# A decoder step on one Trainium2 core: the sample rows' new SSM states formed in the second feed-forward block, and their readout in the mixer from the old states

## The chip, the core and the metric

The kernel runs on one core of a Trainium2 chip. A core has a matmul engine (TensorE, PE in the profile; its weight loads are the row PEld), VectorE (DVE), ScalarE (ACT), GpSimd (POOL) and SyncE (SP), which here issues transfers. Each engine works through its own queue of instructions in order, and engines wait for one another on semaphores. The metric is the device time of one execution in microseconds. Three runs of the kernel before took 1035.49 to 1036.48 us, with a median of 1035.54 us.

## What is computed

One step of a decoder trunk: a half-step SwiGLU feed-forward block, a mixer of two parallel parts (causal pooling, and a Mamba-2 state space part with 16 heads), a second feed-forward block, and a last norm. It runs on 512 prompt rows and on 8 sample rows that each carry a state from earlier steps. Prompt and sample rows are columns of the same tiles: 512 + 8 = 520 columns, in two halves of 260. All inputs and outputs are float32.

```python
def _trunk(x, ...):
    h = h + 0.5 * _swiglu(_rms_norm(h, ffn1_norm[l]), ...)
    m, p, c, s = _hybrid_mixer(_rms_norm(h, mix_norm[l]), ...)
    h = h + m
    h = h + 0.5 * _swiglu(_rms_norm(h, ffn2_norm[l]), ...)
...
def step(h, inp):
    s, a = inp
    return a[..., None, None] * h + s, h
```

For a sample row there is one time step. With its old state h0 (16 heads x 64 x 128), decay a, and the products of the convolved row, the new state is

    h_new = a * h0 + (dt * x) B        (one row of 128 for each of 1024 channels)
    y     = h_new . C                  (sum over the 128)

and y also equals `a * (h0 . C) + (dt * x) * (B . C)`. The new states of all 8 samples are an output (`nss`).

## The kernel before

**Stages.** The first feed-forward block runs to about 400 us of the span, the mixer to about 630, the second block to the end. A scheduler orders each engine's instructions by the program and by what is ready.

**Feed-forward block** (class `Ffn`, L195). The inner dimension of 2816 is 22 tiles f of 128. Gate and up products of a tile are formed by seven products (L264) of split operands; each weight is split into a high part by a cast on ACT (L106) and a low part by a subtraction on DVE (L107), and every product is three matmuls (L116 to L118). One call of `step(f)` (L328) does the products of tile f and the gate of f - 1. Weights of tile f are loaded in `load` (L245) by two SP transfers of 512 KB into one of two raw buffers. After 8, 16 and 22 tiles the down projection runs (`down`, L338, and `down_by_half`, L377), and its result is scaled by `rn`, -0.5 times the reciprocal root mean square, made in `scales` (L302).

**Mixer** (function `mixer`, L541). Its stages are named by letters and run in the order of three written lists (`CONV_PLAN`, `GATE_PLAN`, `LAST_PLAN`, L38 to L46): b and x are projections with a convolution, p the pooling, A and B the prompt's state space part (`ssd_a` L781, `ssd_b` L823), z the gate's projections, G and H the gate and its norm (L875, L886), o, g and h the output projection (L861), and s the samples.

**Samples** (`sample(b, g)`, L758). There are 16 of them: 8 sample rows times 2 groups of 512 channels. B and C of all samples are written to a scratch in DRAM (`sample_bc`, L746). One call then reads B and C of one sample back, broadcast over the 128 partitions (L762); loads 256 KB of old state (L765) into one of two buffers; forms `dt x B` by four copies with a scale per partition on ACT (L769); adds the decayed state by four operations on DVE (L770); stores the new state (L772); and multiplies it by C and sums, by four more operations on DVE (L774), into `ysm`, which `gate` (L875) adds to the prompt's result. A call waits for POOL's last pooling operation (`held["pool"]`, L706 and L909).

**Gate norm** (`gate_out`, L886): for each half of the columns, four squares on ACT (L893), summed over partitions by matmuls with a matrix of ones (L160).

Of the kernel before, what the change touches and what calls it, by code (L numbers as in the profile page):

```python
# [9 lines left out]
F32 = mybir.dt.float32  # L10
F32R = mybir.dt.float32r
AF = mybir.ActivationFunctionType
ALU = mybir.AluOpType
# [3 lines left out]
P = 128  # L17
D = 1024
SEQ = 512
NS = 8  # L20
NT = SEQ + NS
HB = NT // 2
# [10 lines left out]
NX = 8  # L33
# [28 lines left out]
def tile_trunk_step(ctx: ExitStack, tc: tile.TileContext, ins: dict, outs: dict):  # L62
    nc = tc.nc

    def pool(name, side, **kw):
        return tc.alloc_tile_pool(name=name, bufs=1, side=side, reuse_waits="tile", **kw)
# [128 lines left out]
    class Ffn:  # L195
# [3 lines left out]

        def __init__(self, nx, i, wx, gp, direct):  # L200
            self.nx, self.i, self.wx, self.gp, self.direct = nx, i, wx, gp, direct
            self.w, self.A, self.BE, self.ac, self.g, self.tg, self.raw, self.banks, self.behind = ({} for _ in range(9))

        def plain_load(self, f, j=None):
# [96 lines left out]

        def scales(self):  # L302
            rstds(self.nx, f"f{self.i}")
            self.rn = self.wx.tile([P, NT], F32, tag="rn", bufs=1, name=f"rn{self.i}")
            nc.vector.tensor_scalar(out=self.rn, in0=self.nx[3], scalar1=-0.5, scalar2=None, op0=ALU.mult)

        def rest(self, before, last_chunk):
            lo = 0
# [29 lines left out]
        def down(self, c, lo, hi, after):  # L338
            n = hi - lo
            banks, units = {}, {}  # L340

            def part(d, ks):
                if d not in units:
                    units[d] = load_unit(ins[f"w{self.i}d"][d, :, lo * P : hi * P], n * P, f"{self.i}d{d}_{c}")
                    banks[d] = ps[0].tile([P, 2, 512], F32, tag="BE", bufs=2, name=f"dn{self.i}_{d}_{c}")
                wh, wl = units[d]
                for b in range(2):
                    for k in ks:
                        g = self.g[lo + k]
                        mm3(banks[d][:, b, :HB], ws(wh, k), ws(wl, k), g[:, 0, b], g[:, 1, b], k == 0, k == n - 1)  # L350

            def done(d):
                t = self.wx.tile([P, 2, HB], F32, tag="tg", bufs=2, name=f"td{self.i}_{d}_{c}")
                hd = h[:, d].rearrange("p (b t) -> p b t", b=2)
                nc.vector.tensor_tensor(out=t, in0=banks[d][:, :, :HB], in1=self.rn.rearrange("p (b t) -> p b t", b=2),  # L355
                                        op=ALU.mult)
                if after is None:
                    nc.vector.tensor_tensor(out=hd, in0=t, in1=hd, op=ALU.add)
                    return
                for b, hs in enumerate(HALVES):  # L360
                    nc.vector.tensor_tensor(out=h[:, d, hs], in0=t[:, b], in1=h[:, d, hs], op=ALU.add)
                    after(d, b, hs)

            first = 0
            if after is not None:
                part(0, range(n - 1))
                part(1, range(n - 1))
                part(0, range(n - 1, n))
                done(0)
                part(1, range(n - 1, n))  # L370
                done(1)
                first = 2
            for d in range(first, KD):
                part(d, range(n))
                done(d)

        def down_by_half(self, c, lo, after, wd):  # L377
# [25 lines left out]
            def done(d, b):  # L403
                hs = HALVES[b]
                t = self.wx.tile([P, 2, HB], F32, tag="tg", bufs=2, name=f"th{self.i}_{d}{b}")[:, 0]
                nc.vector.tensor_tensor(out=t, in0=banks[d, b][:, :HB], in1=self.rn[:, hs], op=ALU.mult)
# [130 lines left out]
    for p in (ps[0], g2, f2["hg"], f2["wx"]):  # L537
        p.release()


def mixer(tc, ins, outs, e):  # L541
    nc = tc.nc
    cst, act, wp, tmp, dr, pool = (e[x] for x in ("cst", "act", "wp", "tmp", "dr", "pool"))
    bank, load_unit, mm3, ws, v, rstd, rstds, vec, h, nx2, raw_tile, open_f2, fin, fill = (
        e[x] for x in ("bank", "load_unit", "mm3", "ws", "v", "rstd", "rstds", "vec", "h", "nx2", "raw_tile",
                       "open_f2", "fin", "fill"))
# [56 lines left out]
    dv = mp.tile([48, NT], F32, tag="h0", bufs=2, name="dv")  # L603
# [85 lines left out]
    def pooling(g):  # L689
# [16 lines left out]
        held["pool"] = nc.gpsimd.tensor_tensor(out=cur[:, first], in0=cur[:, first], in1=U[:, first], op=ALU.subtract)  # L706
# [21 lines left out]


    sdt = mp.tile([P, NX, NS], F32, tag="sdt", name="sdt")  # L730
    sdec = mp.tile([P, NX, NS], F32, tag="sdec", name="sdec")
    sxdt = mp.tile([P, NX, NS], F32, tag="sxdt", name="sxdt")
    ysm = mp.tile([P, NX, NS], F32, tag="ysm", name="ysm")
    scr_bc = dr.tile([NS, 512], F32, name="scr_bc")

    def sample_decay():
        for j in range(2):
# [8 lines left out]
    def sample_bc():  # L746
        bcs = bank("bcs")
        for j in range(4):
            nc.tensor.transpose(bcs[:NS, j * P : (j + 1) * P], BC[:, j, SEQ:NT], ident)
        bct = mp.tile([NS, 512], F32, tag="ho", bufs=2, name="bct")  # L750
        nc.scalar.copy(bct, bcs[:NS, :])
        nc.sync.dma_start(out=scr_bc, in_=bct)

    def sample_x(g):
        gs = slice(4 * g, 4 * g + 4)
        nc.vector.tensor_tensor(out=sxdt[:, gs], in0=sdt[:, gs], in1=X[:, gs, SEQ:NT], op=ALU.mult)

    def sample(b, g):  # L758
        gs = slice(4 * g, 4 * g + 4)
        shp = [P, 4, P]  # L760
        bcb = mp.tile([P, 2, P], F32, tag="bcb", bufs=2, name=f"bcb{b}{g}")
        nc.sync.dma_start(out=bcb, in_=scr_bc.rearrange("b (a g n) -> b g a n", a=2, g=2)[b, g].unsqueeze(0)  # L762
                          .to_broadcast([P, 2, P]))
        h0 = mp.tile(shp, F32, tag="h0", bufs=2, name=f"h0_{b}{g}")
        nc.sync.dma_start(out=h0, in_=ins["state_ssm"][:, b, gs])  # L765
        o = mp.tile(shp, F32, tag="ho", bufs=2, name=f"ho_{b}{g}")
        for q in range(4):
            j = 4 * g + q
            nc.scalar.activation(out=o[:, q], in_=bcb[:, 0], func=AF.Copy, scale=sxdt[:, j, b : b + 1])  # L769
            nc.vector.scalar_tensor_tensor(out=h0[:, q], in0=h0[:, q], scalar=sdec[:, j, b : b + 1], in1=o[:, q],  # L770
                                           op0=ALU.mult, op1=ALU.add)
        nc.sync.dma_start(out=outs["nss"][:, b, gs], in_=h0)  # L772
        for q in range(4):
            nc.vector.scalar_tensor_tensor(out=o[:, q], in0=h0[:, q], scalar=1.0, in1=bcb[:, 1], op0=ALU.mult,  # L774
                                           op1=ALU.mult, accum_out=ysm[:, 4 * g + q, b : b + 1])


    hst = mp.tile([P, 2, 512], F32, tag="hst", name="hst")
# [96 lines left out]
    def gate(g):  # L875
        zs = zbox[0]
        gs = slice(4 * g, 4 * g + 4)
        with tc.issue_after(held["exp"].ins):
            nc.scalar.activation(out=zs[:, gs], in_=zs[:, gs], func=AF.Silu)
        for q in range(4):  # L880
# [5 lines left out]
    def gate_out(g):  # L886
        zs = zbox[0]
        ry = mp.tile([P, NT], F32, tag="wph", name=f"yr{g}")
        acc = act.tile([P, NT], F32, tag="acc", name=f"yacc{g}")
# [155 lines left out]
```

## Time and profile before

| | us |
|---|---|
| median of three runs (lowest, highest) | 1035.54 (1035.49, 1036.48) |
| the profiled execution | 1034.07 |
| its span, first to last instruction | 1032.3 |
| PE busy in it | 983.7 |
| DVE busy | 809.1 |
| ACT busy | 526.4 |
| POOL busy | 57.8 |

The profile is one execution. "Busy" is the time in which an engine had an instruction running, and matmuls overlap each other, so that a busy PE is not PE at its peak. The granted clock is the share of its full rate at which TensorE was let run. A line of a group reads: source line, engine, operation, output <- inputs, partitions x elements, count, then busy us, mean ns of one, and the idle time of that engine just before them with what ended it. Source lines are those of the kernel before; the changed kernel has other line numbers for the same code.

### The profile page before, as it was taken

What the parts mean: (1) busy time and instruction counts of PE and PEld (TensorE: products, weight loads), DVE (VectorE), ACT (ScalarE), POOL (GpSimd) and SP (SyncE); (2) the same over time, 40 slices, a digit from 0 to 9 for tenths busy, and PEclk for the clock granted to TensorE, in tenths of its full rate; (3) what the DMA queues carried; (4) which work ended last, traced back from release to release, by engine and by line L of the source; (5) the groups of instructions that cost most, each with busy time, mean ns of one, the idle gap of its engine ahead of it and who ended that gap; (6) DMA issues with size and microseconds to landing.
All of it is one profiled execution on the core that took longest, in us unless ns stands there. A gap on an engine that the chain in (4) does not pass through costs nothing.

```text
span 1032.3 us, 19314 instructions
## 1 busy us (share of the span) xinstructions
PE 983.7 (95%) x7848; PEld 958.9 (93%) x7848; DVE 809.1 (78%) x1403; ACT 526.4 (51%) x884; POOL 57.8 (6%) x109
## 2 busy tenths in 40 slices
PE   7999999999999999997798999999999999999984
PEld 6999999999999999997688999899999999999983
DVE  6999557995578787789989877999945899458766
ACT  7566314663145546775585435566622566225452
POOL 0000000000000001338211000000000000000000
PEclk9999999999999999998899999999999999999997
DMA  5333223232231233345444222223223232332213
GB/s 181 115 123 123 83 90 115 83 123 82 96 110 62 89 134 131 130 155 188 127 157 152 95 86 82 83 83 123 83 95 110 83 122 83 99 107 83 92 32 83
DMA packets 45352, 110.25 MB, mean 107 GB/s; under 512 B 5896, under 2 KB 17096, under 8 KB 45264
## 3 DMA queue, kind: packets, MB, share of 16 engines
q1 hardware_dynamic: 45264, 109.03, 31.9%
q8 instruction: 61, 1.00, 0.4%
q14 instruction: 27, 0.22, 0.1%
HBM read 101.67 MB, written 7.34 MB: 106 GB/s over the span
## 4 chain that ended last, share of the span: by engine, by line
PE 80%; DVE 9%; ACT 6%; issue 2%; DMA 2%; SPq 0%; DVEq 0%; ACTq 0%
PE A L116 7%; PE A L117 7%; PE A L118 7%; PE dn L118 7%; PE dn L116 7%; PE dn L117 7%; PE BE L116 6%; PE BE L118 5%; PE BE L117 5%; PE P L228 3%; PE wo L116 2%; PE wo L118 2%; PE wo L117 2%; PE inz L116 1%; PE inz L117 1%
## 5 line engine op out<-in xcount | busy, mean ns | idle before, releaser
L355 DVE TENSOR_TENSOR td<-dn,rn 128x520 f32<-128x520 f32 x40 | 27.9, 699 | 113.2 <-PE dn L118 113.2
L116 PE MATMUL dn<-g,whi_1d 128*128 128x260 f32 x352 | 99.5, 283 | 1.7 <-ACT whi_1d L106 1.5
L117 PE MATMUL dn<-g,whi_1d 128*128 128x260 f32 x352 | 99.3, 282 | 0.0
L118 PE MATMUL dn<-g,wlo_1d 128*128 128x260 f32 x352 | 99.2, 283 | 0.0
L116 PE MATMUL dn<-g,whi_2d 128*128 128x260 f32 x256 | 72.5, 283 | 1.6 <-ACT whi_2d L106 1.6
L117 PE MATMUL dn<-g,whi_2d 128*128 128x260 f32 x256 | 72.4, 283 | 0.0
L118 PE MATMUL dn<-g,wlo_2d 128*128 128x260 f32 x256 | 72.3, 284 | 0.0
L116 PEld LDWEIGHTS dn<-g,whi_1d 128*128 128x128 f32 x352 | 66.2, 188 | 2.4 <-ACT whi_1d L106 2.0
L117 PEld LDWEIGHTS dn<-g,whi_1d 128*128 128x128 f32 x352 | 66.3, 188 | 0.0
L118 PEld LDWEIGHTS dn<-g,wlo_1d 128*128 128x128 f32 x352 | 66.2, 188 | 0.0
L284 ACT COPY ac<-A 128x260 f32<-128x260 f32 x123 | 45.9, 373 | 37.7 <-PE A L118 36.1
L106 ACT CAST whi_1d<-raw_1d 128x1024 fp32r<-128x1024 f32 (+1 forms) x24 | 23.4, 979 | 73.0 <-PE dn L117 63.0
L106 ACT CAST whi_2d<-raw_2d 128x1024 fp32r<-128x1024 f32 (+1 forms) x19 | 19.3, 1018 | 68.4 <-PE dn L117 59.3
L228 PE MATMUL P<-xg_f,raw 128*128 128x260 f32 x192 | 45.9, 397 | 5.7 <-DMA raw<-in_w1gu 5.7
L116 PEld LDWEIGHTS dn<-g,whi_2d 128*128 128x128 f32 x256 | 48.4, 189 | 2.0 <-ACT whi_2d L106 2.0
L256 DVE TENSOR_TENSOR s<-raw 128x1024 f32<-128x1024 f32 x41 | 50.0, 1219 | 0.0
L117 PEld LDWEIGHTS dn<-g,whi_2d 128*128 128x128 f32 x256 | 48.3, 189 | 0.0
L228 PEld LDWEIGHTS P<-xg_f,raw 128*128 128x128 f32 x192 | 37.4, 199 | 11.6 <-ACT sq_f L154 5.7
L118 PEld LDWEIGHTS dn<-g,wlo_2d 128*128 128x128 f32 x256 | 48.1, 189 | 0.0
L116 PE MATMUL inz<-xh_mx,whi_inz 128*128 128x260 f32 x128 | 37.7, 294 | 0.0
L116 PE MATMUL wo<-catg,whi_wo 128*128 128x260 f32 x128 | 37.5, 293 | 0.2 <-DVE h L869 0.2
L116 PE MATMUL inx<-xh_mx,whi_inx 128*128 128x260 f32 x128 | 37.4, 292 | 0.0
(1326 smaller groups left out, 3933.9 us busy)
## 6 DMA issues: line engine op xcount, KB each, us to landing
raw<-in_w2gu SPq DMA_DIRECT2D x44, 512.0 KB, 3.8
raw<-in_w1gu SPq DMA_DIRECT2D x42, 512.0 KB, 4.4
raw_1d<-in_w1d SPq DMA_DIRECT2D x16, 512.0 KB, 3.9
raw_2d<-in_w2d SPq DMA_DIRECT2D x16, 512.0 KB, 4.1
raw_wo<-in_w_out SPq DMA_DIRECT2D x12, 512.0 KB, 4.7
h<-in_state_ssm SPq DMA_DIRECT2D x16, 256.0 KB, 4.4
ab<-scr_acs SPq DMA_DIRECT2D x8, 512.0 KB, 5.1
out_nss<-h SPq DMA_DIRECT2D x16, 256.0 KB, 3.0
```

The source lines that it names most:

```text
L106: nc.scalar.copy(h, src)
L116: nc.tensor.matmul(ps, whi, xhi, start=start, stop=False, **kw)
L117: nc.tensor.matmul(ps, whi, xlo, start=False, stop=False, **kw)
L118: nc.tensor.matmul(ps, wlo, xhi, start=False, stop=stop, **kw)
L228: nc.tensor.matmul(self.banks[f, u][b][:, :HB], ws(self.raw[f][:, u], j + 4 * q), xg[:, slot[q]], start=j == q == 0, stop=j == 3 and q == ...
L256: nc.vector.tensor_tensor(out=s1, in0=diag, in1=up0, op=ALU.add)
L284: nc.scalar.copy(keep, out[:, :HB])
L355: nc.vector.tensor_tensor(out=t, in0=banks[d][:, :, :HB], in1=self.rn.rearrange("p (b t) -> p b t", b=2), op=ALU.mult)
```

## The change

The samples' work is cut in two.

In the mixer, `sample(b, g)` loads C alone (64 KB where B and C were 128 KB) and the old state (now four buffers, before two), and multiplies the *old* state by C on DVE, four operations with a sum, into `ysm`. All 64 of these write their products into one scratch tile, `junk`. A new `sample_y(g)` makes y from it: `ysm * sdec + sxdt * (B . C)`, three operations on tiles of 128 x 32 for each of the two groups. The numbers B . C of all samples come from one product on DVE, one matmul with ones and one copy in `sample_bc`. The wait for POOL's pooling is gone.

The new states are formed in `new_states(wx)`, a generator. `Ffn.step(f)` of the second block advances it once for each f over 2. One turn starts the next sample's loads (B, and the old state for a second time), then forms `dt x B` by four scaled copies on ACT, scales the old state in place by four more on ACT, adds the one to the other by a transfer that accumulates, issued by POOL, and stores the result by a transfer on SP.

Three smaller edits: `rn` is gone, and the factor -0.5 is part of the operation that scales the down projection (a `scalar_tensor_tensor` where a `tensor_tensor` was); `gate_out` squares whole tiles of 520 columns into the no longer needed X, where it squared halves into temporary tiles; `sdec` and `sxdt` live in the pool of constants, so that they outlive the mixer.

```diff
+            self.states = None
...
         def scales(self):
             rstds(self.nx, f"f{self.i}")
-            self.rn = self.wx.tile([P, NT], F32, tag="rn", bufs=1, name=f"rn{self.i}")
-            nc.vector.tensor_scalar(out=self.rn, in0=self.nx[3], scalar1=-0.5, scalar2=None, op0=ALU.mult)
...
         def step(self, f):
+            if self.states is not None and f > 2:
+                next(self.states, None)
...
-                nc.vector.tensor_tensor(out=t, in0=banks[d][:, :, :HB], in1=self.rn.rearrange("p (b t) -> p b t", b=2),
-                                        op=ALU.mult)
+                nc.vector.scalar_tensor_tensor(out=t, in0=banks[d][:, :, :HB], scalar=-0.5,
+                                               in1=self.nx[3].rearrange("p (b t) -> p b t", b=2), op0=ALU.mult,
+                                               op1=ALU.mult)
...
+    f2["st"] = pool("st2", "left")
+    f2["ffn"].states = f2["states"](f2["st"])
...
+        dots = bank("dots")[:, : 2 * NS]
+        nc.vector.tensor_tensor(out=sbc, in0=BC[:, 0:2, SEQ:NT], in1=BC[:, 2:4, SEQ:NT], op=ALU.mult)
+        nc.tensor.matmul(dots, ones, sbc.rearrange("p g b -> p (g b)"), start=True, stop=True)
+        nc.scalar.copy(sbc, dots.rearrange("p (g b) -> p g b", g=2))
...
     def sample(b, g):
+        cb = tmp.tile([P, HB], F32, tag="ta", name=f"cb{b}{g}")[:, :P]
+        nc.sync.dma_start(out=cb, in_=rows_bc(b, 1, g))
+        h0 = mp.tile([P, 4, P], F32, tag="h0", bufs=4, name=f"h0_{b}{g}")
+        nc.sync.dma_start(out=h0, in_=ins["state_ssm"][:, b, 4 * g : 4 * g + 4])
+        for q in range(4):
+            nc.vector.scalar_tensor_tensor(out=junk, in0=h0[:, q], scalar=1.0, in1=cb, op0=ALU.mult, op1=ALU.mult,
+                                           accum_out=ysm[:, 4 * g + q, b : b + 1])
+
+    def sample_y(g):
         gs = slice(4 * g, 4 * g + 4)
-        for q in range(4):
-            j = 4 * g + q
-            nc.scalar.activation(out=o[:, q], in_=bcb[:, 0], func=AF.Copy, scale=sxdt[:, j, b : b + 1])
-            nc.vector.scalar_tensor_tensor(out=h0[:, q], in0=h0[:, q], scalar=sdec[:, j, b : b + 1], in1=o[:, q],
-                                           op0=ALU.mult, op1=ALU.add)
-        nc.sync.dma_start(out=outs["nss"][:, b, gs], in_=h0)
-        for q in range(4):
-            nc.vector.scalar_tensor_tensor(out=o[:, q], in0=h0[:, q], scalar=1.0, in1=bcb[:, 1], op0=ALU.mult,
-                                           op1=ALU.mult, accum_out=ysm[:, 4 * g + q, b : b + 1])
+        xb = mp.tile([P, 4, NS], F32, tag="xb", name=f"xb{g}")
+        nc.vector.tensor_tensor(out=xb, in0=sxdt[:, gs], in1=sbc[:, g : g + 1].to_broadcast([P, 4, NS]), op=ALU.mult)
+        nc.vector.tensor_tensor(out=ysm[:, gs], in0=ysm[:, gs], in1=sdec[:, gs], op=ALU.mult)
+        nc.vector.tensor_tensor(out=ysm[:, gs], in0=ysm[:, gs], in1=xb, op=ALU.add)
+
+    def new_states(wx):
+        def load(b, g):
+            br = wx.tile([P, P], F32, tag="sb", bufs=2, name=f"br{b}{g}")
+            nc.sync.dma_start(out=br, in_=rows_bc(b, 0, g))
+            hs = wx.tile([P, 4, P], F32, tag="sh", bufs=2, name=f"hs{b}{g}")
+            nc.sync.dma_start(out=hs, in_=ins["state_ssm"][:, b, 4 * g : 4 * g + 4])
+            return br, hs
+
+        todo = [(b, g) for g in range(2) for b in range(NS)]
+        ahead = load(*todo[0])
+        for i, (b, g) in enumerate(todo):
+            yield
+            br, hs = ahead
+            if i + 1 < len(todo):
+                ahead = load(*todo[i + 1])
+            o = wx.tile([P, 4, P], F32, tag="so", bufs=2, name=f"so{b}{g}")
+            for q in range(4):
+                j = 4 * g + q
+                nc.scalar.activation(out=o[:, q], in_=br, func=AF.Copy, scale=sxdt[:, j, b : b + 1])
+                nc.scalar.activation(out=hs[:, q], in_=hs[:, q], func=AF.Copy, scale=sdec[:, j, b : b + 1])
+            nc.gpsimd.dma_start(out=hs, in_=o, accum_op=ALU.add)
+            nc.sync.dma_start(out=outs["nss"][:, b, 4 * g : 4 * g + 4], in_=hs)
...
     def gate_out(g):
+        for q in range(4):
+            nc.scalar.activation(out=X[:, 4 * g + q], in_=zs[:, 4 * g + q], func=AF.Square)
         for b, hs in enumerate(HALVES):
-            sq = [acc[:, hs]] + [tmp.tile([P, HB], F32, tag="ta", name=f"ysq{g}{q}{b}") for q in range(1, 4)]
-            for q in range(4):
-                nc.scalar.activation(out=sq[q], in_=zs[:, 4 * g + q, hs], func=AF.Square)
-            rstd(ry, sq, hs, 512, f"y{g}{b}")
+            rstd(ry, [X[:, 4 * g + q, hs] for q in range(4)], hs, 512, f"y{g}{b}")
...
-                with tc.issue_after(held["pool"].ins):
-                    sample(*smp.pop(0))
+                sample(*smp.pop(0))
```

More of the change, by code (lines that the diff above doesn't have):

```diff
@@ L405, in done @@
                 t = self.wx.tile([P, 2, HB], F32, tag="tg", bufs=2, name=f"th{self.i}_{d}{b}")[:, 0]
-                nc.vector.tensor_tensor(out=t, in0=banks[d, b][:, :HB], in1=self.rn[:, hs], op=ALU.mult)
+                nc.vector.scalar_tensor_tensor(out=t, in0=banks[d, b][:, :HB], scalar=-0.5, in1=self.nx[3][:, hs],
+                                               op0=ALU.mult, op1=ALU.mult)
                 nc.vector.tensor_tensor(out=h[:, d, hs], in0=t, in1=h[:, d, hs], op=ALU.add)
@@ L536, in tile_trunk_step @@
     f2["ffn"].rest(before2, after2)
-    for p in (ps[0], g2, f2["hg"], f2["wx"]):
+    for p in (ps[0], f2["st"], g2, f2["hg"], f2["wx"]):
         p.release()
@@ L543, in mixer @@
     cst, act, wp, tmp, dr, pool = (e[x] for x in ("cst", "act", "wp", "tmp", "dr", "pool"))
+    ones = e["ones"]
     bank, load_unit, mm3, ws, v, rstd, rstds, vec, h, nx2, raw_tile, open_f2, fin, fill = (
@@ L602, in mixer @@
     rstds(nx2[0], "mx")
-    dv = mp.tile([48, NT], F32, tag="h0", bufs=2, name="dv")
+    dv = mp.tile([48, NT], F32, tag="h0", bufs=4, name="dv")
     for b, hs in enumerate(HALVES):
@@ L705, in pooling @@
         nc.gpsimd.tensor_tensor(out=cur[:, first], in0=cur[:, first], in1=rcnt[:, : w - 1], op=ALU.mult)
-        held["pool"] = nc.gpsimd.tensor_tensor(out=cur[:, first], in0=cur[:, first], in1=U[:, first], op=ALU.subtract)
+        nc.gpsimd.tensor_tensor(out=cur[:, first], in0=cur[:, first], in1=U[:, first], op=ALU.subtract)
         nc.gpsimd.tensor_copy(npp[:, g], U[:, SEQ : SEQ + PAST])
@@ L730, in mixer, with rows_bc @@
     sdt = mp.tile([P, NX, NS], F32, tag="sdt", name="sdt")
-    sdec = mp.tile([P, NX, NS], F32, tag="sdec", name="sdec")
-    sxdt = mp.tile([P, NX, NS], F32, tag="sxdt", name="sxdt")
+    sdec = cst.tile([P, NX, NS], F32, tag="sdec", name="sdec")
+    sxdt = cst.tile([P, NX, NS], F32, tag="sxdt", name="sxdt")
     ysm = mp.tile([P, NX, NS], F32, tag="ysm", name="ysm")
+    sbc = mp.tile([P, 2, NS], F32, tag="sbc", name="sbc")
+    junk = act.tile([P, NT], F32, tag="acc", name="junk")[:, :P]
     scr_bc = dr.tile([NS, 512], F32, name="scr_bc")
+    def rows_bc(b, a, g):
+        return scr_bc.rearrange("b (a g n) -> b a g n", a=2, g=2)[b, a, g].unsqueeze(0).to_broadcast([P, P])
     def sample_decay():
@@ L749, in sample_bc @@
             nc.tensor.transpose(bcs[:NS, j * P : (j + 1) * P], BC[:, j, SEQ:NT], ident)
-        bct = mp.tile([NS, 512], F32, tag="ho", bufs=2, name="bct")
+        bct = mp.tile([NS, 512], F32, tag="h0", bufs=4, name="bct")
         nc.scalar.copy(bct, bcs[:NS, :])
         nc.sync.dma_start(out=scr_bc, in_=bct)
+        dots = bank("dots")[:, : 2 * NS]
+        nc.vector.tensor_tensor(out=sbc, in0=BC[:, 0:2, SEQ:NT], in1=BC[:, 2:4, SEQ:NT], op=ALU.mult)
+        nc.tensor.matmul(dots, ones, sbc.rearrange("p g b -> p (g b)"), start=True, stop=True)
+        nc.scalar.copy(sbc, dots.rearrange("p (g b) -> p g b", g=2))
     def sample_x(g):
@@ L758, in sample @@
     def sample(b, g):
-        gs = slice(4 * g, 4 * g + 4)
[L760 to L766, printed above, removed]
@@ L778, in mixer @@
+    e["f2"]["states"] = new_states
     hst = mp.tile([P, 2, 512], F32, tag="hst", name="hst")
@@ L877, in gate @@
         gs = slice(4 * g, 4 * g + 4)
+        sample_y(g)
         with tc.issue_after(held["exp"].ins):
@@ L888, in gate_out @@
         ry = mp.tile([P, NT], F32, tag="wph", name=f"yr{g}")
-        acc = act.tile([P, NT], F32, tag="acc", name=f"yacc{g}")
+        for q in range(4):
+            nc.scalar.activation(out=X[:, 4 * g + q], in_=zs[:, 4 * g + q], func=AF.Square)
         for b, hs in enumerate(HALVES):
-            sq = [acc[:, hs]] + [tmp.tile([P, HB], F32, tag="ta", name=f"ysq{g}{q}{b}") for q in range(1, 4)]
-            for q in range(4):
-                nc.scalar.activation(out=sq[q], in_=zs[:, 4 * g + q, hs], func=AF.Square)
-            rstd(ry, sq, hs, 512, f"y{g}{b}")
+            rstd(ry, [X[:, 4 * g + q, hs] for q in range(4)], hs, 512, f"y{g}{b}")
         cat = cats[g] = xa.tile([P, 2, 4, NT], F32R, tag="xa", bufs=2, name=f"catg{g}")
```

## The prediction

> **What bounds the kernel now.** First the busy times, the clock row and the shares of the chain, on the page:
>
> ```profile
> PE 983.7 (95%) x7848; PEld 958.9 (93%) x7848; DVE 809.1 (78%) x1403; ACT 526.4 (51%) x884; POOL 57.8 (6%) x109
> PEclk9999999999999999998899999999999999999997
> PE 80%; DVE 9%; ACT 6%; issue 2%; DMA 2%; SPq 0%; DVEq 0%; ACTq 0%
> ```
>
> TensorE sets the time nearly everywhere; only around slices 20 to 22 of 40 does its clock dip, and there the chain goes over VectorE and ScalarE. So I read the busy times in stretches of 5 us there (PE, weight load, DVE, ACT, POOL, clock, DMA share, GB/s):
>
> ```profile
> 465.00:470.00 5.00, 5.00 (x44) 5.00 (x44) 5.00 (x9) 2.22 (x5) 5.00 (x5) 1.00 0.59 193
> 470.00:475.00 5.00, 2.06 (x13) 1.23 (x11) 5.00 (x15) 2.20 (x5) 2.80 (x7) 0.94 0.63 233
> 475.00:480.00 5.00, 4.82 (x29) 4.49 (x30) 5.00 (x17) 3.87 (x11) 3.48 (x5) 0.50 0.07 27
> 490.00:495.00 5.00, 1.03 (x2) 0.50 (x2) 5.00 (x11) 1.28 (x4) 1.82 (x5) 0.65 0.30 90
> 540.00:545.00 5.00, 2.06 (x13) 1.23 (x11) 5.00 (x8) 4.97 (x15) 2.85 (x3) 1.00 0.29 74
> ```
>
> A full stretch holds 44 matmuls. DVE is full while PE starves, and after each hole the granted clock is low for some 5 us. Over the sixteen stretches of 470 to 550, PE is busy 62.7 of 80 us (17.3 idle) and does 479 matmuls where 704 fit: about 25 us lost, 8 of them to the clock (a little less, since a few of these matmuls are 512 wide). This is all the mixer can return. The groups that the change touches there:
>
> ```profile
> L770 DVE SCALAR_TENSOR_TENSOR h<-h,sdec,ho 128x128 f32<-128x128 f32 x64 | 20.4, 365 | 4.6 <-ACT ho L769 2.7 <-ACT A L667 1.9
> L769 ACT ACTIVATE ho<-bcb,sxdt 128x128 f32<-128x128 f32 x64 | 20.4, 390 | 18.5 <-DMA bcb<-scr_bc 18.3
> L774 DVE SCALAR_TENSOR_TENSOR ho<-h,bcb 128x128 f32<-128x128 f32 x64 | 20.2, 352 | 0.0
> ```
>
> Then the place that receives the work: two steps of the second feed-forward block in the same columns, and from the timeline one weight cast there and the matmul that first uses it (start, duration):
>
> ```profile
> 691.94:702.04 10.10, 10.10 (x86) 10.10 (x85) 9.55 (x14) 6.25 (x10) 0.00 (x0) 1.00 0.31 113
> 732.34:742.44 10.10, 10.10 (x86) 10.10 (x85) 9.37 (x14) 6.44 (x10) 0.00 (x0) 1.00 0.32 101
> ```
>
> ```profile
> 742.44 1.05 ACT L106 CAST whi_9a<-raw 128x1024 fp32r<-128x1024 f32 x1 [0.88 <-PE A L117]
> 746.67 0.28 PE L116 MATMUL A<-xth_f,whi_9a 128*128 128x260 f32 x1
> ```
>
> A step takes 10.1 us, PE full, ACT busy 6.4. Casts run ahead of their matmul by little: this one ends at 743.5 and is used at 746.67, 3.2 us of slack.
>
> **The change in the mixer.** Gone: 64 updates on DVE. In a row of six they cost 1.66 us, so 0.28 each; the windows put 52 of them before 550 us: 14.6 us. Gone too: 64 products on ACT and its 18.3 us of waiting for broadcasts, and 16 stores. Added on DVE: one product of B and C and six small operations, 0.19 each by the like row of DVE's timeline, L756 (128x32): 1.3 us. The readouts now share one scratch tile, so each waits for the one before; two dependent operations (L669) take 1.57 us where an independent pair is 0.09 shorter, and about 20 of the 64 stand next to each other: 2 us. Net 11 us less DVE work in the stretch where DVE is full. That fills 11 of the 17.3 idle us and its part of the clock loss (8 x 11/17.3 = 5): 16, of which I take 15, since DVE now waits for the broadcasts itself, where ACT did. Bounds: 8 (net 11 less 3 for such waits) and 25 (all that PE lost).
>
> Taken at nothing: the sum over partitions and its copy (like psr_y, 0.38 us, among full PE work); the squares, 16 halves become 8 whole ones (ACT, under w_out matmuls, PE full from 550 to 625; uncovered, the first sum waits some 2 us more for four whole squares); the scale -0.5 folded into the eviction (0.42 us by either form at 128x260, L239 against L406; DVE waits 113 us for these matmuls anyway), and the 0.42 us that made the scaled tile.
>
> **The change in the second block.** Added: 128 ACT copies, 16 POOL-issued accumulating transfers, and on SP's queue 16 broadcasts, 16 state loads and 16 stores. The text asks for one sample a step, but in the changed kernel's built order all 16 stand in steps 2 to 9, two a step. Per step: ACT has so, so, then hs (four copies each), the second hs right ahead of the next weight cast; SP has store, store, load, broadcast, load, broadcast, then the weights. The stores wait for the accumulation, the loads into the same two buffers wait for the stores, hs on ACT waits for the load, and POOL waits for hs. It is a loop, and the weight casts, their gates and SP's weight loads queue behind it.
>
> ```profile
> h<-in_state_ssm SPq DMA_DIRECT2D x16, 256.0 KB, 4.4
> out_nss<-h SPq DMA_DIRECT2D x16, 256.0 KB, 3.0
> raw<-in_w2gu SPq DMA_DIRECT2D x44, 512.0 KB, 3.8
> scr_dt<-dts SPq DMA_DIRECT2D x1, 0.5 KB, 1.3
> q1 hardware_dynamic: 45264, 109.03, 31.9%
> ```
>
> ```profile
> 526.24 1.26 ACT ho L769 x4
> ```
>
> The first four are transfers with their us from issue to landing; q1 is the only queue that carries the kernel's own data, so no POOL-issued transfer is in this trace; the last is four ACT copies in a row on the chain of waits. The accumulation's time X is unknown. Below, any transfer: 1.3. Above, a read and a write one after the other: 4.4 + 3.0 = 7.4. I take 4.4, the row of the same 256 KB read. By the Trainium skill (DMA: Bandwidth & Descriptors, "Anatomy of one DMA — SWDGE (gpsimd) path") such a transfer takes 2.0 us plus its bytes at 436 GB/s, 2.6 here as an estimate; no run here shows it yet, and the sum by it would be 1033.
>
> Loop: X 4.4 + store 3.0 + load 3.6 (below 4.4, as the DMA engines are 31% busy here and 512 KB takes 3.8) + four copies 1.3 + issues 0.4 = 12.7 us. ACT alone needs 6.4 + 16 x 0.315 = 11.4 us for a step with two samples. Both exceed 10.1, so the step is max(11.4, X + 8.3). Start, in times of before: the loads are issued behind those of 665.6, the first pair's copies end at 675.7 and 678.2 between the step's own; +4.4 accumulated at 680.1, +3.0 stored 683.1, second store issued behind the reload 683.5, landed 686.5, reload landed 690.2, copied 691.5. Six more pairs follow: 691.5 + 6 x 12.7 = 767.7, where the cast behind the last one began at 742.4: 25.3 late, less 3.2 of slack: PE loses 22 us. In general 6 x max(11.4, X + 8.3) + X - 58.5: 11 at X = 1.3, 43 at 7.4. Later steps cannot win it back, as PE is full in them.
>
> **Sum.** The profiled execution took 1034.07 us (span 1032.3 and 1.8 around it), 1.5 under the median 1035.54. 1034.07 - 15 + 22 = 1041; on the median, 1042 to 1043: I say 1042.
>
> **Rivals.**
> 1. *The accumulation is quick.* At X = 3.0, the row of a 256 KB store, ACT's work sets the step: PE loses 6 x 11.4 + 3.0 - 58.5 = 13 us, and the mixer's 15 to 20 outweighs it: about -5, 1031, faster. It decides at X of about 3.4 (6 x 11.7 + 3.4 - 58.5 = 15). For it: the bytes are few and these transfers find the engines two thirds free. Against: it reads two operands and lands before it may be stored. Chance 0.27. The Trainium skill's 2.6 us, in the section named above, lies on this side.
> 2. *DVE stays the mixer's bound.* Readouts now wait in DVE's order for cb and state loads (four and three buffers, where ACT waited 18.3 us for the like). The mixer returns 5: 1052. Against: loads are issued two or three samples ahead. 0.15.
> 3. *The accumulation is slow*, X = 7.4: 1034.07 - 15 + 43 + 1.5 = 1063 or so. For it: it reads both operands before it writes, and no row shows what POOL needs to set one up. 0.10.
> 4. *The change does what its text says*, one sample a step: ACT needs 8.9 of 10.1 us and the loop has two steps' time; only the start costs some 3: 1035.5 - 15 + 3 = 1023. Against: the built order is fixed. 0.03.
>
> **How the numbers follow.** Forecast 0.45, rivals 0.27, 0.15, 0.10, 0.03. Faster by over 0.2% (2 us, about what the runs can tell from no change): rival 4 and most of rival 1, with the forecast's cases of a mixer gain near 25: 0.27. Within 0.2%: where loss and gain meet, 0.10. Slower: the rest, 0.63. Range 1028 to 1057: from rival 1 with a little more gain to past rival 2; left out are most of 3 and 4. The forecast's own, with X from 3.8 to 5.2 and a gain of 10 to 20: 1033 to 1053.
>
> **What would show it.** POOL-issued transfers land in 4.4 us; ACT waits in the second block for the state loads, and SP for accumulations; PE idles there some 22 us in holes of 2 to 3 us from 680 on, for some 85 us, with its clock below full. In the mixer PE's idle time falls from 17 to about 6 us. I am wrong if X is under 3.4, if ACT waits for nothing new in steps 2 to 9, or if PE still idles for DVE as before.

## The result, and the profile after

The changed kernel took 1047.29 us (median of 4 runs, 1045.96 to 1051.1) beside 1036.0 us for the kernel before on the same chip: a ratio of 1.0115, with a 95% interval of 1.0086 to 1.0144. Slower, as forecast, by 11 us where 6 to 7 were forecast. The profiled execution took 1048.36 us (span 1045.8), 14.3 more than the one of before.

First the page of the kernel after: busy times, clock row, shares of the chain by engine.

```profile
PE 987.7 (94%) x7850; PEld 961.5 (92%) x7850; DVE 795.3 (76%) x1344; ACT 540.0 (52%) x941; POOL 71.8 (7%) x125
PEclk9999999999999999998999999989999999999996
PE 78%; DMA 8%; DVE 5%; ACT 5%; issue 3%; SPq 0%; POOL 0%; DVEq 0%; POOLq 0%; ACTq 0%
```

DVE has 14 us less to do, ACT 14 us more, and the chain now goes over transfers. Of the two low slices of the clock at the mixer (the 19th and 20th; the prediction counted them as 20 to 22) one is left, and a new one, the 27th, stands at 680 to 706 us, where the second block runs its first steps.

The mixer, in the same kind of view as before (stretches of 5 us: PE, weight load, DVE, ACT, POOL, clock, DMA share, GB/s):

```profile
475.00:480.00 5.00, 5.00 (x44) 5.00 (x43) 5.00 (x13) 3.11 (x4) 3.88 (x4) 1.00 0.12 36
...
490.00:495.00 5.00, 2.69 (x12) 2.33 (x13) 5.00 (x14) 5.00 (x13) 2.94 (x4) 0.55 0.44 142
540.00:545.00 5.00, 5.00 (x44) 5.00 (x43) 5.00 (x17) 2.87 (x7) 1.05 (x1) 1.00 0.35 141
```

One large hole is left, from 480 to 495, with DVE still full in it. Over 470 to 550 PE is busy 72.4 of 80 us (7.6 idle, 17.3 before). Read as one stretch, it does 579 matmuls there instead of 459: 120 more, and at the 0.118 us of full stretches that is 14 us won. (Stretches of 5 us count a matmul that crosses an edge twice; their sums are 611 and 479.)

The second block, in stretches of 10 us:

```profile
680.00:690.00 10.00, 5.96 (x34) 5.75 (x33) 5.79 (x9) 7.57 (x22) 0.85 (x1) 0.75 0.73 201
...
710.00:720.00 10.00, 8.64 (x59) 8.64 (x60) 7.16 (x11) 7.62 (x18) 1.71 (x2) 0.83 0.86 221
...
730.00:740.00 10.00, 7.01 (x55) 6.59 (x54) 7.16 (x9) 7.54 (x18) 0.86 (x1) 0.98 0.73 195
```

A full stretch holds 85 matmuls; these have 34 to 59, and neither ACT nor DVE is full in them. The loss can be read off SP's weight loads, first of the kernel before, then of the kernel after (start, duration):

```profile
665.59 0.33 SPq L249 DMA_DIRECT2D raw<-in_w2gu  x1
...
783.07 0.33 SPq L249 DMA_DIRECT2D raw<-in_w2gu  x1
```

```profile
651.34 0.33 SPq L250 DMA_DIRECT2D raw<-in_w2gu  x1
...
794.46 0.33 SPq L250 DMA_DIRECT2D raw<-in_w2gu  x1
```

The loads of f = 3 were issued at 665.59 us before and 651.34 after, 14.3 earlier: the mixer's gain. Those of f = 10, behind the last step with samples, came at 783.07 and 794.46: 117.5 us on the way before, 143.1 after, so 25.6 lost (27.8 by the end, as the span grew by 13.5 in spite of the 14.3). The first of the steps with samples takes 21.3 us by these loads, the next five 12.7 to 13.9, where a step took 10.1.

What the steps wait for, from the chain of waits of 640 to 770 us (start, length, what):

```profile
700.39 6.72 DMA hs<-so
707.17 2.01 DMA out_nss<-hs
709.27 2.86 DMA hs<-in_state_ssm
712.25 2.04 issue
714.30 5.77 DMA hs<-so
```

It is the loop of the forecast, going round: accumulate, store, reload into the same buffer, scale (the "issue" piece), accumulate again; 13.9 us for this turn and 14.1 for the next (to 728.36), two samples in each. The waits of 630 to 800 us agree (in total, times, longest), SP first and then ACT:

```profile
SPq L811 <- DMA hs<-so: 61.6, 15, 8.7
```

```profile
ACT so L808 <- DMA hs<-so: 9.6, 5, 3.0
ACT hs L809 <- DMA hs<-in_state_ssm: 6.1, 6, 1.8
```

### The profile page after: what moved, and what is told of

The parts are those of the page before. It is cut to its first block, busy times and chain, and to the rows that moved or that the text cites. A ratio compares the mean times of both kernels' runs of the same rounds, so it can differ in the third digit from the quotient of the medians.

```text
span 1045.8 us, 19435 instructions
## 1 busy us (share of the span) xinstructions
PE 987.7 (94%) x7850; PEld 961.5 (92%) x7850; DVE 795.3 (76%) x1344; ACT 540.0 (52%) x941; POOL 71.8 (7%) x125
## 3 DMA queue, kind: packets, MB, share of 16 engines
q0 software_dynamic: 2304, 4.20, 2.2%
## 4 chain that ended last, share of the span: by engine, by line
PE 78%; DMA 8%; DVE 5%; ACT 5%; issue 3%; SPq 0%; POOL 0%; DVEq 0%; POOLq 0%; ACTq 0%
PE dn L116 7%; PE dn L118 7%; PE dn L117 7%; PE A L116 6%; PE A L117 6%; PE A L118 6%; PE BE L116 5%; PE BE L118 5%; PE BE L117 5%; DMA hs<-so 3%; PE wo L116 2%; PE wo L118 2%; PE wo L117 2%; PE P L229 2%; DMA out_nss<-hs 2%
## 5 line engine op out<-in xcount | busy, mean ns | idle before, releaser
L356 DVE SCALAR_TENSOR_TENSOR td<-dn,r_f 128x520 f32<-128x520 f32 x40 | 27.9, 699 | 113.6 <-PE dn L118 113.6
L117 PE MATMUL inz<-xl_mx,whi_inz 128*128 128x260 f32 x128 | 36.9, 288 | 0.0
```

The costliest lines, as they stand in the source:

```text
L117: nc.tensor.matmul(ps, whi, xlo, start=False, stop=False, **kw)
L356: nc.vector.scalar_tensor_tensor(out=t, in0=banks[d][:, :, :HB], scalar=-0.5, in1=self.nx[3].rearrange("p (b t) -> p b t", b=2), op0=ALU.mult,
```

## The experiments

Every kernel was timed beside the kernel before on the same chip; since chips differ (before: 1033.0 to 1036.0), the ratios are what to compare. In the diffs, lines begin with - for the changed kernel and + for the experiment. One thing makes them harder to read: the build plans the order of each engine anew, so an edit of one line can also move the samples' work. Where it does, the text says so.

**The mixer's half alone.** The new states are not formed at all.

```
-    f2["ffn"].states = f2["states"](f2["st"])
```

> The mixer's half alone: the samples' new states are not formed (this part of the computation is left out), all else is as in the changed kernel. If the two halves add, as I read the two traces (raw_3's load issued 14.2 us earlier, then lost again and more in the second block): 1036 - 14 = 1022 us, PE full in the second block. If the mixer gave less and the earlier start was given back elsewhere (the halves of the first sum, the folded -0.5): 1030 or more.

1023.45 us, ratio 0.9892 (0.9877 to 0.9908): 12 us won, where 14 were expected. The rest of the change, the second block, then costs 1.0115 - 0.9892 = 2.2%, 23 us. In its trace 116.7 us lie between the weight loads of f = 3 and f = 10, against 143.1: 26. This kernel is the floor for what follows.

**One sample a step.** All parts of the change are kept, but a sample's copies on ACT stand behind the Silu of the step before.

```
-                next(self.states, None)
+                with tc.issue_after(self.silu):
+                    next(self.states, None)
```

> Every part of the change stays, but a sample's copies on ACT are held behind the Silu of the step before, so that one sample stands in each step. Theory 1 (two samples a step in a loop over two buffers): the loop has a whole step per sample, ACT needs 6.4 + 8 x 0.315 = 8.9 of 10.1 us; the second block loses some 3 us: 1025, faster than both kernels. Rival (accumulating transfers cost PE or the weight loads time whatever their spacing, 27 / 16 = 1.7 us each): 1045 to 1050.

1032.41 us, 0.9972 (0.9958 to 0.9987): 15 us better than the changed kernel and just faster than before. One stretch of this kernel:

```profile
690.00:700.00 10.00, 10.00 (x86) 10.00 (x85) 9.21 (x14) 9.11 (x20) 1.90 (x2) 1.00 0.55 165
```

From 670 to 730 PE is full with accumulations, stores and reloads going on beside it; what is lost lies mostly where the gate-and-up steps end (PE busy 8.7 of 10 us from 730 to 740) and begin again (8.4 from 800 to 810). So the transfers do not cost PE time by being there, when they are spaced like this. But 8 us over the floor is more than the 3 expected.

**Without the accumulation.**

```
-            nc.gpsimd.dma_start(out=hs, in_=o, accum_op=ALU.add)
```

> The accumulating transfer is left out: the stored states lack dt.x.B; all ACT copies, loads and stores remain. Theory 1 (the loop of copies, accumulation, store and reload sets the 13 us step): the loop falls to about 7 us, ACT's own work is left, 6 x 11.4 - 58.5 = 10 us at most, so 1022 + 10 = 1032 us or less, and the stores no longer wait on SP. Theory 2 (ACT's added work alone holds the weight casts): the copies are all still there, 1045 us, a step of 13. Theory 3 (SP's weight loads behind 48 more transfers): all but 16 remain, about 1043.

1047.53 us, 1.0134 (1.011 to 1.0159): no better. Theory 1 as I had put it falls, and theory 2 by its number stands; but the order was not the same. With no accumulation to wait for, the build put three samples into a step, and ACT became full (one stretch of 10 us; 690 to 700 is the same):

```profile
680.00:690.00 10.00, 6.68 (x40) 6.05 (x39) 6.51 (x9) 10.00 (x29) 0.00 (x0) 0.83 0.67 191
```

By ACT's own work a step with three samples takes 6.4 + 24 x 0.315 = 14.0 us, and the weight loads of the three full steps of this kind stand 14.9, 13.8 and 16.0 us apart. So ACT's work is a second bound close behind the loop, and taking the accumulation away uncovers it. ACT's work is not alone here, though: from 710 to 730 ACT is busy 7.5 to 8.4 of 10 us, and the chain of waits still holds a reload of 5.3 us and a store of 5.7, each issued right behind weights on SP's queue.

**Without the scaling.** Here the other side is taken away: ACT has half of the added copies.

```
-                nc.scalar.activation(out=hs[:, q], in_=hs[:, q], func=AF.Copy, scale=sdec[:, j, b : b + 1])
```

> The four copies that scale the old state by its decay are left out (the stored states lack the decay), half of the added ACT work; loop, accumulation, loads and stores remain. Theory 1 (the loop): it shortens only by the four copies, 13.1 - 1.3 = 11.8 us a step, against 13.1: the loss falls from 27 to about 18, 1040 us. Theory 2 (ACT's work): 6.4 + 8 x 0.315 = 8.9 us a step, under 10.1, no loss left: 1025.

1058.06 us, 1.0216 (1.0186 to 1.0247): worse than either theory had it, and against ACT's work as the bound, which fell from 11.4 to 8.9 us a step. The waits of 640 to 810 us in this kernel:

```profile
POOL hs L809 <- DMA hs<-in_state_ssm: 46.4, 8, 9.3
ACT so L808 <- DMA hs<-so: 32.2, 9, 7.9
```

In this order the `so` copies stand ahead of the step's own evictions and casts, and wait for a free `so` buffer, that is for the accumulation of two samples before (32.2 us, 9.6 in the changed kernel). ACT stands idle there up to 7.9 us with casts queued behind it. There are still two samples in most steps. The loop, with little work on ACT, costs 34 us over the floor; but it is a longer loop than the changed kernel's, since two of its reloads stand just behind weights on SP's queue and take 6.3 and 7.4 us on its chain (2.7 to 2.9 in the changed kernel).

**What the transfer itself costs.** First the same transfer, overwriting instead of adding. The order of the instructions on ACT, SP, DVE and POOL is exactly that of the changed kernel.

```
-            nc.gpsimd.dma_start(out=hs, in_=o, accum_op=ALU.add)
+            nc.gpsimd.dma_start(out=hs, in_=o)
```

> The transfer from so to hs overwrites instead of adding (the stored states are dt.x.B alone, without the old state); the instructions and their order on every engine are those of the changed kernel. If the adding makes the transfer long (5.5 us; its queue held 13.8% of the DMA engines' time for 4.20 MB, the other queue 43.4% for 24.05 MB, 1.8 times as much for a byte): the copy lands in about 3 us, the pair's loop falls from 13.1 to 10.6, ACT's 11.4 us then sets the step, 6 x 11.4 + 3 - 58.5 = 13 us lost: 1023 + 13 = 1036 us. If a transfer issued from POOL is as long whatever it does: 1047.

1043.19 us, 1.0098 (1.008 to 1.0116), against 1.0115 (1.0086 to 1.0144): the totals can't be told apart. The traces can. From the DMA issues on the page of this kernel (KB each, median us from issue to landing):

```profile
hs<-so POOLq DMA_DIRECT2D x16, 256.0 KB, 4.3
```

On POOL's timeline the first transfer of a pair and that of the pair six turns of the loop later, for the copy and then in the changed kernel (start, duration, ..., idle before and what ended it):

```profile
674.47 0.54 POOL L810 DMA_DIRECT2D hs<-so  x1 [7.39 <-ACT ac L285]
...
750.12 0.54 POOL L810 DMA_DIRECT2D hs<-so  x1 [9.82 <-ACT ac L285]
```

```profile
673.10 0.86 POOL L810 DMA_DIRECT2D hs<-so  x1 [7.63 <-ACT ac L285]
...
754.74 0.86 POOL L810 DMA_DIRECT2D hs<-so  x1 [10.28 <-ACT ac L285]
```

That is 12.6 us a turn for the copy, 13.6 for the accumulation. The copy lands 1.2 us sooner (4.3 for 5.5), and the turn is 1.0 shorter: the step follows the transfer nearly one for one, as max(11.4, X + ...) says while X is above its turning point. The weight loads of f = 3 and f = 10 agree: 137.0 us apart for the copy, 143.1 in the changed kernel. The ratios show less than these 6 us (0.17% is 2 us, with intervals that leave room for some 5), so this reading rests on one trace of each kernel. The expected 3 us for a copy was wrong, so 11.4 was not reached.

Then a quarter of the bytes:

```
-            nc.gpsimd.dma_start(out=hs, in_=o, accum_op=ALU.add)
+            nc.gpsimd.dma_start(out=hs[:, :1], in_=o[:, :1], accum_op=ALU.add)
```

> The accumulating transfer carries one of a sample's four tiles, 64 KB for 256 (three quarters of the stored states lack dt.x.B); copies, loads and stores as in the changed kernel, about two samples a step. If its time goes with its bytes: it lands in some 3 us against 5.5, the pair's loop is 7.7 + 3 = 10.7, ACT's 11.4 sets the step: 1036 or less, and POOL's issues stand 11.4 us apart. If most of it is a fixed time: it lands in 4.5 or more, issues 12.2 or more apart, 1042 to 1046.

```profile
hs<-so POOLq DMA_DIRECT2D x16, 64.0 KB, 4.5
```

64 KB land in 4.5 us, 256 KB in 5.5: as far as two kernels with different orders can be compared, most of it is a fixed time, as the second case had it. The kernel counts as much as the size: the same 256 KB accumulation landed in 4.3 us in the median with one sample a step, and in 6.2 in the kernel with three buffers between the down projections, below. POOL's issues for a pair stood 11.4 to 13.7 us apart, so they fit neither case alone. The total, 1053.85 us (1.0169, 1.0154 to 1.0185), is outside both: this build has the samples in another order (SP mostly issues single stores and reloads in turn where it had pairs, and the reload's share of the chain from 650 to 770 us is 21% where it was 10%), so the total says nothing on the transfer.

**Another place.** The samples' turns are moved between the units of the down projections, where ACT and DVE have room; DVE scales and adds in one operation.

```
-            if self.states is not None and f > 2:
-                next(self.states, None)
...
+                if self.states is not None:
+                    with tc.issue_after(cast[0]):
+                        for _ in range(2 if d == 0 else 1):
+                            next(self.states, None)
...
-                nc.scalar.activation(out=hs[:, q], in_=hs[:, q], func=AF.Copy, scale=sdec[:, j, b : b + 1])
-            nc.gpsimd.dma_start(out=hs, in_=o, accum_op=ALU.add)
+                nc.vector.scalar_tensor_tensor(out=hs[:, q], in0=hs[:, q], scalar=sdec[:, j, b : b + 1], in1=o[:, q],
+                                               op0=ALU.mult, op1=ALU.add)
```

> A sample's turn is taken between the units of the two down projections instead of the gate-and-up steps, and VectorE scales the old state and adds so in one operation of four (no accumulating transfer, no scaling copies). ACT is busy 2 of 10 us there and VectorE 4 to 6, so 8 x 1.3 us of each fit in 50: the mixer's half stays whole: 1024 us, faster than both kernels. If the 48 transfers beside the weight loads cost time anywhere they stand (some 0.5 us a sample): 1032.

1024.02 us, 0.991 (0.9894 to 0.9926): the fastest of those that form the whole states, 0.9% under before, 2% under the changed kernel, and 0.2% over the floor, with intervals that overlap. One of its stretches:

```profile
760.00:770.00 10.00, 10.00 (x85) 10.00 (x84) 6.88 (x14) 3.96 (x10) 0.00 (x0) 1.00 0.52 183
```

PE is full, DVE and ACT have room, and the DMA engines are busy (0.52 here, 0.71 in the stretch ahead of it) nearly as in the changed kernel's steps. Next, the same place with the change's own copies and accumulation:

```
-                nc.vector.scalar_tensor_tensor(out=hs[:, q], in0=hs[:, q], scalar=sdec[:, j, b : b + 1], in1=o[:, q],
-                                               op0=ALU.mult, op1=ALU.add)
+                nc.scalar.activation(out=hs[:, q], in_=hs[:, q], func=AF.Copy, scale=sdec[:, j, b : b + 1])
+            nc.gpsimd.dma_start(out=hs, in_=o, accum_op=ALU.add)
```

(- is the kernel just above.)

> As the kernel with the turns between the down projections' units, but with the change's own work: eight ACT copies and the accumulating transfer of a sample. The loop is as long as before (13 us for two samples, 6.5 us a unit against units of some 6 us), but few casts stand behind it there. If place is what costs: 1025 to 1029. If the accumulating transfers cost time by themselves: 1040 or more.

1042.08 us, 1.0086 (1.0072 to 1.01): 18 us over the other form, so the place alone does not cure it. ACT is idle more than half of the time there, and still waits, as its timeline shows (start, length, ..., idle before and what ended it):

```profile
784.68 1.28 ACT L813 ACTIVATE hs<-hs,sdec 128x128 f32<-128x128 f32 x4 [6.16 <-DMA hs<-in_state_ssm]
```

6.2 us of waiting for a reload, with the next weight cast behind it. POOL's issues are 16.4 and 14.4 us apart for two samples, against units of some 6 us for one. This kernel with three buffers in place of two:

```
-            br = wx.tile([P, P], F32, tag="sb", bufs=2, name=f"br{b}{g}")
+            br = wx.tile([P, P], F32, tag="sb", bufs=3, name=f"br{b}{g}")
...
-            hs = wx.tile([P, 4, P], F32, tag="sh", bufs=2, name=f"hs{b}{g}")
+            hs = wx.tile([P, 4, P], F32, tag="sh", bufs=3, name=f"hs{b}{g}")
...
-            o = wx.tile([P, 4, P], F32, tag="so", bufs=2, name=f"so{b}{g}")
+            o = wx.tile([P, 4, P], F32, tag="so", bufs=3, name=f"so{b}{g}")
```

> The turns between the down projections' units, with the change's own eight ACT copies and accumulating transfer, and three buffers in place of two for br, hs and so. If the loop through two buffers (copies, accumulation, store, reload: some 14 us for two samples there, against units of 6 us) is what cost the 1042 of the form with two: three samples share a loop, 5 us each, and it falls to 1024 to 1030. If accumulating transfers cost time by themselves, or SP's weight loads behind the stores that wait for them: it stays near 1042.

1035.14 us, 1.0007 (0.9994 to 1.0021): 8 of the 18 us back. The loop was one part; the trace shows the other at the end of the projection, in DVE's and SP's timelines:

```profile
784.43 1.23 DVE L259 TENSOR_TENSOR s<-raw 128x1024 f32<-128x1024 f32 x1 [7.63 <-DMA raw<-in_w2gu]
```

```profile
774.22 0.42 SPq L252 DMA_DIRECT2D raw<-in_w2gu  x1
776.95 0.33 SPq L799 DMA_DIRECT2D hs<-in_state_ssm  x1
...
777.88 0.49 SPq L253 DMA_DIRECT2D raw<-in_w2gu  x1
```

The second half of the pair of weights is issued 3.7 us behind the first, since a reload between them waits for a store; DVE waits 7.6 us for it, and evictions stand behind DVE. Weight loads behind stores and reloads in SP's order, theory 3 above, are thus a real cost here.

**Three buffers where the change has two**: the same three lines, in the changed kernel.

> The changed kernel with three buffers in place of two for br, hs and so, and nothing else; in its built order ACT then has three samples in most of steps 2 to 6. Theory 1 in full (a step is the longer of the loop and ACT's own work): the loop for three samples is still 13 us and ACT needs 6.4 + 24 x 0.315 = 14.0 us, over five to six steps: 20 to 23 us lost, 1043 to 1046, hardly better. The loop alone: its time for a sample falls from 6.5 to 4.4 us, 1032 to 1036.

1058.42 us, 1.0231 (1.0211 to 1.025): 12 us worse than with two. SP's stores show three or four samples in most steps, the loop turns in 16 to 18 us (POOL's issues at 677.28, 694.95, 710.83), and PE's clock is at 0.66 to 0.83 in every stretch of 10 us from 680 to 730. My sum, 14.0 us of ACT work for a step with three samples, had too few of them and left out that waits come on top: ACT is 57 to 89% busy there.

**DVE adds, one sample a step.** The edit of the spaced form, and this one:

```
-                nc.scalar.activation(out=hs[:, q], in_=hs[:, q], func=AF.Copy, scale=sdec[:, j, b : b + 1])
-            nc.gpsimd.dma_start(out=hs, in_=o, accum_op=ALU.add)
+                nc.vector.scalar_tensor_tensor(out=hs[:, q], in0=hs[:, q], scalar=sdec[:, j, b : b + 1], in1=o[:, q],
+                                               op0=ALU.mult, op1=ALU.add)
```

> One sample a step as in the kernel that gave 1032, but VectorE scales and adds (four operations more a step, some 1.2 us, where VectorE is busy 9.3 of 10.1 us), and ACT has four copies a step fewer. If the 9 us that the spaced form still lost lie in ACT's and the transfer's work: 1026. If VectorE becomes the bound of the step (9.3 + 1.2 = 10.5 us against 10.1, over 16 steps): 1023 + 7 = 1030 or more.

1029.19 us, 0.9956 (0.9941 to 0.997). DVE is at 10.00 of 10 us in 710 to 720 and from 810 to 850 again: it is the bound, as the second case had it.

**DVE adds, in the change's own place**: the edit just above alone.

> In the changed kernel's own place (two to three samples in steps 2 to 7), VectorE scales the old state and adds; no accumulating transfer, four ACT copies a sample. If the accumulating loop is what cost the 24 us over the mixer's half: 1026 to 1030. If a step overfull on its engines costs as much (VectorE 9.3 + 2.5 x 4 x 0.28 = 12.1 us against 10.1, over six steps 12 us, ACT 6.4 + 2.5 x 1.26 = 9.6): 1035.

1052.79 us, 1.0163 (1.0146 to 1.0179): worse than the changed kernel, without any accumulation. That refutes the reading that the accumulation by itself is the cause. The chain of waits, 650 to 770 us:

```profile
688.77 5.90 DMA out_nss<-hs
694.69 3.00 DMA hs<-in_state_ssm
...
704.39 7.12 DMA out_nss<-hs
711.53 2.97 DMA hs<-in_state_ssm
```

There is still a loop: the reload into one of two buffers waits for the store from it, and a store issued right behind the weights takes 5.9 to 7.1 us (2.0 in the changed kernel's median, 3.2 in this one's). And DVE, which has the weights' splits to do, now waits for reloads itself (14.9 us from 640 to 800).

Those that form the whole states, beside the floor, by ratio to before:

| kernel | samples' place | state formed by | ratio (95%) |
|---|---|---|---|
| mixer's half alone | none | - | 0.9892 (0.9877-0.9908) |
| down projections | 1 a unit | ACT, DVE | 0.9910 (0.9894-0.9926) |
| DVE adds, spaced | 1 a step | ACT, DVE | 0.9956 (0.9941-0.9970) |
| spaced | 1 a step | ACT, accumulation | 0.9972 (0.9958-0.9987) |
| down projections, 3 buffers | 1 a unit | ACT, accumulation | 1.0007 (0.9994-1.0021) |
| down projections | 1 a unit | ACT, accumulation | 1.0086 (1.0072-1.0100) |
| the changed kernel | 2 a step | ACT, accumulation | 1.0115 (1.0086-1.0144) |
| DVE adds | 3 to 4 a step | ACT, DVE | 1.0163 (1.0146-1.0179) |
| 3 buffers | 3 to 4 a step | ACT, accumulation | 1.0231 (1.0211-1.0250) |

## Why the prediction held, step by step

- **The mixer's 15.** By the weight loads 14.3, by the count of matmuls 14, by the kernel with that half alone 12. Idle time fell from 17.3 to 7.6 us where I had named about 6. DVE hardly waits for its broadcasts (the readouts: 1.8 us), so the 1 us taken off for that was about right, and rival 2 (the mixer returns 5) is out. The price of the one scratch tile is there too: readouts in a row start 0.33 us apart (469.22, 469.54 and 469.87 us) where they started 0.21 apart before (476.19, 476.40 and 476.61). Over the whole kernel DVE's busy time fell by 13.8 us, where 64 x 0.28 - 1.3 - 2 = 14.6 by the terms of the sum. (The 479 of 704 matmuls in the prediction count those on the edges of stretches twice; counted once they are 459 of some 680, which makes 26 us lost where the prediction has 25.)
- **What was taken at nothing** stays without a visible price: the new scaling in the eviction takes 0.70 us as the old form did (L356 against L355), and PE is full from 600 to 650. It was not tested one by one.
- **The second block's 22.** It lost 25.6 by the weight loads, 23 by the ratios. The mechanism is the one forecast; the sizes in the loop were off both ways. In the term "X 4.4", X was 5.5 in the median and 5.8 to 6.7 on the chain. Store 3.0 and load 3.6 were 2.0 to 3.3 and 2.7 to 2.9. Copies and issues, 1.3 + 0.4, were 2.0. A turn took 13.6 for the 12.7 of the sum. Against the kernel with the mixer's half alone, whose weight loads are 12.4 and then 10.0 us apart, the first step lost 9 (21.3 for 12.4; ACT is busy 9.99 of 10 us from 660 to 670 with its copies) and the next five 16.5 (66.5 for 50.0). My sum had six turns of 2.6 too long, 15.6, and some 6 for the start.
- **max(11.4, X + 8.3).** Each side was seen to hold the steps in a kernel of its own, though not alone there: the loop with little ACT work (34 us lost), ACT's work with no accumulation (25 us lost). That the loop is the longer one in the changed kernel rests on its chain of waits and on the copy that landed 1.2 us sooner and turned 1.0 us faster. X = 3.1, under which ACT's work would set the step by this formula, was reached by no kernel's median here, so the 11.4 us for two samples was never the longer side.
- **A wait that I had not named.** With two `so` buffers, the `so` copies wait for the accumulation of two samples before. I had the hs copies wait on ACT; the `so` copies waited longer (9.6 us against 6.1), and in the kernel without scaling this wait is the main one.
- **What would show it.** Holes for some 100 us from 660 on, where 85 from 680 were named. But PE's idle time grew by 17 us there (18.1 us between 660 and 770, against 1.3 in the kernel with the mixer's half alone), not 22; the count of matmuls, 686 against 897 there, makes 25 us at 0.118, so about 8 went to the clock (0.75 to 0.91 in four of the stretches), which I had not told apart from idle time.
- **Rivals.** 1 falls by X: 5.5, and even the plain copy has 4.3. The estimate of 2.6 us, from the 2.0 us plus the bytes at 436 GB/s of the Trainium skill (DMA: Bandwidth & Descriptors, "Anatomy of one DMA — SWDGE (gpsimd) path"), does not hold in this kernel: 4.3 copied, 5.5 accumulated, and the measurement decides. 3 falls too: 7.4 is among the longest single ones (up to 7.8), far from the median. 4 was run as a kernel of its own: 1032 where I had worked out 1023, since it cost 8 rather than 3 over the mixer's half, and that half gave 12 rather than 15; in the changed kernel two samples a step were built, as its order said.

That the 22 came out so near is in part luck. X was 1.1 us larger than taken, while store and load were up to 1.0 and 0.9 smaller, and five steps behind the first were drawn out where the sum had six turns.

What stays open: how much of the loss each of the three (the loop, ACT's own work, weight loads behind stores on SP) would keep if the other two were gone, in the change's own place. Each edit there that took one of them away moved the order too.

## What to carry to other kernels

Work that is taken off a full engine has to fit where it goes in every queue it enters: here 40 us of copies on an ACT that was busy 6.4 of 10.1 us became a loop through two buffers, four engines and the queue of the weights, and each turn of 13.6 us stood in the way of a step of 10.1. Before moving work, write down such a loop (load, scale, add, store, reload) and compare its turn with the step of the place; then look at the built order for how many of them share a step. The cure was not a faster part of the loop but a place with room and work spread over it: one sample a unit of the down projections, formed on ACT and DVE, keeps nearly all that the mixer won (0.991 of before).

## What the runs showed of the hardware that I had not expected

- An accumulating transfer of 256 KB between two tiles, issued from POOL, took 5.5 us to land in the median of the changed kernel, and the same transfer without adding 4.3 in the same order of instructions. In other kernels the accumulation took 4.3 to 6.2, and one with a quarter of the bytes 4.5. POOL itself was busy 0.86 us for an issue, and 0.54 without adding.
- For the same 4.20 MB, the accumulating form took 2304 packets and 2.2% of the DMA engines' time in the changed kernel, the plain copy 1280 and 1.0%. With a quarter of the bytes the accumulating form took 2304 packets as well.
- A 256 KB store took 2.0 us in the median of the changed kernel, and 5.9 to 7.1 in the kernel where DVE adds in the change's own place, when it was issued right behind 1 MB of weights on the same queue. Reloads of 256 KB just behind weights took 6.3 and 7.4 us in the kernel without scaling, where 2.7 to 2.9 was usual in the changed kernel.
